# A hybrid encoder block: twelve late tiles of its input projection as six pairs of seven products

## The chip, the cores and the metric

The kernel runs on one core of a Trainium2 chip. The metric is the device time of one launch in microseconds (us), as the median of several runs. The engines are named as the profile names them: PE is TensorE's matmuls and PEld its weight loads, DVE is VectorE, ACT is ScalarE, POOL is GpSimd, SP issues most DMAs. A suffix q (SPq) is the engine's queue.

## The reference, cut to what matters

```python
hn = rmsnorm(concat(meta_tokens, x), norm_in_g)      # 16 + 512 rows, 2048 wide
P = hn @ w_in                                        # 2048 x 8320: r, k, v, g, two low ranks, B, C, h, gc
Pr = Pr + (prev - Pr) * mu_shift                     # r, k, v, g and the low ranks only
y = rwkv7_recurrence(r, decay, k, v, kk, kk * a)     # 16 heads of 64, chunks of 64 frames
y_a = (groupnorm(y) + bonus) * silu(g)
y_b = B * causal_conv3(C * h) * silu(gc)             # 1024 channels
out = rmsnorm(h_res + concat(y_a, y_b) @ w_out, norm_f_g)[16:]
```

Everything is float32.

## The kernel before

**The input projection.** Weights are cut into 65 tiles of 128 output columns: one for the low ranks, eight each of r, k, v, g, B, C, h and gc. `plan` lists them in the order in which TensorE takes them; the last sixteen are C, h, B, gc for i = 4 to 7. Float32 products are made from float32r parts: a value is split into a high part (a cast) and a low part (the value less its high part), and three matmuls, high x high, high x low and low x high, stand for one product. The activations, scaled by the norm's gain, lie split in `xh` and `xl`, 16 blocks (kt) of 128 inputs by 528 frames. One tile is 16 blocks by three matmuls for every range of frames (`steps`, L346). B and gc take the 512 real frames in one matmul; C and h need two frames more for the convolution and take them as 258 + 256 columns.

**Weights.** A tile is loaded as two halves of 512 KB (`prefetch`, L166) into a ring of three `raw` buffers. A half is two quarters of 512 columns. `split_w` makes a quarter's parts: ScalarE casts (L158), VectorE or GpSimd subtracts (L159; of every half one quarter each, from the twelfth half on). The parts go to a ring of six buffers, `hl`.

**The order.** TensorE's order is written out by hand. `mains` is a generator that yields after every matmul of the projection; the recurrence and what prepares it call `fill(ns)`, which takes matmuls from it for as many ns as the kernel counts (0.43 ns a column). So every step of the recurrence is followed by projection matmuls that fill the time until its result is there; the lengths stand in the table `FW`. `later(ns, fn)` puts off DMA issues by the same clock. The order on VectorE, ScalarE and GpSimd is the framework's scheduler's, with `tc.high_priority` and `tc.issue_after` as hints; each engine then runs its own list in order.

**Recurrence.** For pairs of heads, `prepare` and `invert` make the operands of the chunked recurrence, and `recur` runs nine chunks. In a chunk z (L996) goes through ScalarE as pn (L1004), is multiplied again (L1013), copied as u by ScalarE and VectorE (L1016, L1017), and gives outputs and the next state (L1048, L1052; L1060 and L1061 on VectorE). The fills behind the three steps are p, u and s. `norm` normalises a chunk's output (L1077 to L1089, with a power on GpSimd, L123).

**The end.** After the recurrence, `split_mix` loads and gates the 16 tiles of the mix (L1141) and splits them (L1146, L1147), and `sums` (L1157 to L1160) makes sums of its quarters, between the last four tiles of the projection. The output projection (L1285) is made of seven products of quarter matrices instead of eight, in the form of Strassen and Winograd: the sums of the mix on one side (`split_form`, L1202 and L1203), sums of the weights on the other (`add`, L1246, or by DMA), split by `split_unit` (L1255, L1256).

## Time and profile before

| | |
|---|---|
| median of three runs | 1000.38 us (1000.17 to 1001.08) |
| the profiled execution | 1001.71 us, span 999.9 us |
| PE, PEld busy | 988.3, 911.6 us |
| DVE, ACT, POOL busy | 685.7, 394.6, 271.5 us |
| DMA | 174.8 MB, mean 175 GB/s |
| mean granted TensorE clock | 0.997 |

Times in the views are us from the span's start. A group's row gives the line, the engine, the operation, output<-inputs with their shapes, the count, then busy time in us and the mean of one instruction in ns, then the engine's idle time in front and what ended it. A timeline row gives start, length and instruction. Matmuls overlap in the array, so that one lasts longer than its distance to the next.

### The profile page before, as it was taken

How to read it: one execution, taken by the hardware profiler on the slowest of the kernel's cores; microseconds unless marked ns; L12 is line 12 of the kernel's file. 1: busy time of each engine (PE TensorE's matmuls, PEld its weight loads, DVE VectorE, ACT ScalarE, POOL GpSimd, SP SyncE). 2: the span in 40 equal slices, each digit the busy share in tenths (PEclk: the TensorE clock that was granted, in tenths of full speed). 3: DMA queues.
4: the chain of work that ended last, by engine and by line, in shares of the span. 5: the costliest groups of instructions: out<-in, count | busy, mean ns of one | idle time of the engine just before them, and what ended most of it. 6: DMA issues, size and time to landing. Idle time of an engine off the chain costs nothing.

```text
span 999.9 us, 23699 instructions
## 1 busy us (share of the span) xinstructions
PE 988.3 (99%) x9723; PEld 911.6 (91%) x9723; DVE 685.7 (69%) x1247; ACT 394.6 (39%) x729; POOL 271.5 (27%) x292
## 2 busy tenths in 40 slices
PE   9999999999999999999999999999999999999996
PEld 7999999999998999998999998889889898888885
DVE  6777965588765679744669644244554697997897
ACT  7553433344313434322434322222232426546463
POOL 0122423234233424232324222223332333001001
PEclk9999999999999999999999999999999999999998
DMA  9525576555575373854274846877673688797654
GB/s 329 148 85 148 132 207 171 153 144 145 141 189 165 95 193 98 203 149 119 85 197 108 197 136 192 297 215 241 204 226 99 174 264 210 187 318 175 160 127 168
DMA packets 185036, 174.82 MB, mean 175 GB/s; under 512 B 121568, under 2 KB 142816, under 8 KB 184416
## 3 DMA queue, kind: packets, MB, share of 16 engines
q1 hardware_dynamic: 182336, 164.40, 57.2%
q0 software_dynamic: 2304, 8.39, 4.8%
q8 instruction: 76, 1.25, 0.5%
q10 hardware_dynamic: 288, 0.52, 0.1%
q14 instruction: 32, 0.26, 0.1%
HBM read 136.92 MB, written 36.35 MB: 173 GB/s over the span
## 4 chain that ended last, share of the span: by engine, by line
PE 90%; DVE 5%; DMA 2%; issue 1%; SPq 0%; ACT 0%; POOL 0%; DVEq 0%; ACTq 0%; POOLq 0%
PE ps_v L346 9%; PE ps_k L346 9%; PE ps_h L346 9%; PE ps_g L346 9%; PE ps_r L346 9%; PE ps_B L346 9%; PE ps_gc L346 9%; PE ps_C L346 8%; PE M L1285 5%; PE P L1285 2%; DVE o L1256 2%; PE g L703 2%; PE Q L1285 1%; PE zs L1048 1%; PE ps_lora L346 1%
## 5 line engine op out<-in xcount | busy, mean ns | idle before, releaser
L158 ACT CAST w<-wr 128x512 fp32r<-128x512 f32 x252 | 153.0, 619 | 285.4 <-PE ps_C L346 47.3
L159 POOL TENSOR_TENSOR w<-wr,w 128x512 fp32r<-128x512 f32 x119 | 169.1, 1422 | 346.6 <-ACT w L158 289.4
L159 DVE TENSOR_TENSOR w<-wr,w 128x512 fp32r<-128x512 f32 x133 | 98.6, 747 | 114.5 <-ACT w L158 114.2
L346 PE MATMUL ps_k<-xh,w 128*128 128x272 f32 (+1 forms) x512 | 95.3, 284 | 0.0
L346 PE MATMUL ps_v<-xh,w 128*128 128x256 f32 (+1 forms) x512 | 95.3, 284 | 0.0
L346 PE MATMUL ps_r<-xh,w 128*128 128x258 f32 (+1 forms) x512 | 94.4, 281 | 0.0
L346 PE MATMUL ps_h<-xh,w 128*128 128x256 f32 (+1 forms) x512 | 94.0, 282 | 0.0
L346 PE MATMUL ps_C<-xh,w 128*128 128x256 f32 (+1 forms) x512 | 93.1, 281 | 0.0
L346 PE MATMUL ps_g<-xh,w 128*128 128x256 f32 (+1 forms) x512 | 91.5, 280 | 0.0
L346 PE MATMUL ps_B<-xh,w 128*128 128x512 f32 x256 | 83.8, 395 | 0.0
L346 PE MATMUL ps_gc<-xh,w 128*128 128x512 f32 x256 | 81.3, 392 | 0.0
L346 PEld LDWEIGHTS ps_k<-xh,w 128*128 128x128 f32 x512 | 80.0, 188 | 0.4
L346 PEld LDWEIGHTS ps_v<-xh,w 128*128 128x128 f32 x512 | 80.0, 188 | 0.3
L346 PEld LDWEIGHTS ps_h<-xh,w 128*128 128x128 f32 x512 | 79.2, 188 | 0.7
L346 PEld LDWEIGHTS ps_r<-xh,w 128*128 128x128 f32 x512 | 79.6, 188 | 0.1
L346 PEld LDWEIGHTS ps_C<-xh,w 128*128 128x128 f32 x512 | 79.2, 188 | 0.6
L346 PEld LDWEIGHTS ps_g<-xh,w 128*128 128x128 f32 x512 | 78.7, 188 | 0.2
L346 PE MATMUL ps_k<-xl,w 128*128 128x272 f32 (+1 forms) x256 | 72.6, 284 | 0.0
L346 PE MATMUL ps_v<-xl,w 128*128 128x272 f32 (+1 forms) x256 | 72.5, 283 | 0.0
L346 PE MATMUL ps_h<-xl,w 128*128 128x258 f32 (+1 forms) x256 | 71.8, 281 | 0.5 <-issue 0.5
L346 PE MATMUL ps_g<-xl,w 128*128 128x258 f32 (+1 forms) x256 | 72.0, 281 | 0.0
L346 PE MATMUL ps_r<-xl,w 128*128 128x258 f32 (+1 forms) x256 | 72.0, 281 | 0.0
(337 smaller groups left out, 2265.3 us busy)
## 6 DMA issues: line engine op xcount, KB each, us to landing
wr<-in_w_in_dram SPq DMA_DIRECT2D x126, 512.0 KB
ct<-opd SPq DMA_DIRECT2D x64, 288.0 KB
wo<-in_w_out_dram SPq DMA_DIRECT2D x24, 512.0 KB
x<-in_w_out_dram POOLq DMA_DIRECT2D x16, 512.0 KB, 6.1
opd<-ar SPq DMA_DIRECT2D x8, 576.0 KB
opd<-gt SPq DMA_DIRECT2D x16, 288.0 KB
opd<-bt SPq DMA_DIRECT2D x64, 64.0 KB
x<-in_w_out_dram SPq DMA_DIRECT2D x8, 512.0 KB
```

Source lines behind the costliest of these rows:

```text
L158: nc.scalar.copy(hi, rq)
L159: low[q] = eng.tensor_tensor(out=lo, in0=rq, in1=hi.bitcast(F32), op=ALU.subtract).ins
L346: nc.tensor.matmul(ps[r], ww[:, w], xx[:, kt, a:b], start=(kt == 0 and n == 0), stop=(kt == KT - 1 and n == 2))
L703: nc.tensor.matmul(z[h][:, c - c0], bk[hs, c, h : h + 2, :].rearrange("p a s -> p (a s)"), ar[hs, c].rearrange("p a s -> p (a s)"), start= ...
L1048: nc.tensor.matmul(d[hs, j], w, x[hs], start=(a == 0), stop=(a == b - 1))
L1256: last = nc.vector.tensor_tensor(out=lo, in0=rq, in1=hi.bitcast(F32), op=ALU.subtract)
L1285: nc.tensor.matmul(bank[s], left(prod, jj, m, s), w, start=(jj == 0 and n == 0), stop=(jj == 7 and n == 2))
```

## The change

Of the last sixteen tiles, C, h, B and gc for i = 4 to 6 are taken as six pairs, (C, h) and (B, gc). A pair is a product of 2 x 2 quarters: two tiles of outputs, two halves of the 2048 inputs, two halves of the 512 frames. Instead of eight products of quarters, seven are made, each of 8 blocks by 256 or 258 frames: M1, P5, Q6, M3, M7, M2, P4. Four of them have sums of weight quarters, made in place in the raw buffers; four have sums of activations. Banks of PSUM are used twice within a pair: after M1 its value is copied out and Q6 is added onto it, and so on. The results are put together from the copies and banks by ScalarE and VectorE.

The activation sums are made early in the projection, one block of eight after the other, stored in DRAM (`fsum`), and loaded and split before the recurrence. The third of them (M7's) is written over the second half of frames in `xh` and `xl` for the first eight blocks (`third_form`), and undone after the last M7 (`restore`). For that the frames lie in two segments, with two frames twice.

Beside that: `raw` becomes four named buffers in pairs; parts of the weights in a pair are dealt out to VectorE and GpSimd by a table, and after the last pair all low parts of the input weights are GpSimd's; the product and first tap of the convolution go to VectorE for i from 4 on; both copies u go to ScalarE and overwrite pn; several buffers of the recurrence are single instead of double; the fills p, u and s are shorter; in the output projection some form splits are put behind weight splits on VectorE; the framework's scheduler is asked to order by its timeline (`schedule_with_timeline_sim=True`); the mix stage begins once `restore` is issued.

```diff
-    tr=3200, ..., p=2900, u=2900, s=5200, last=3700, mix=2600,
+    tr=3200, ..., p=2300, u=2500, s=4200, last=3700, mix=2600, form=1000, split=6000, early=60000, apart=48000,
...
+ON_POOL = {   # (low part, sum): which halves of a product's weights GpSimd makes
+    "M1": ((), ()), "P5": ((), ()), "Q6": ((), ()), "M3": ((0, 1), ()), "M7": ((0, 1), (0, 1)), "M2": ((0, 1), ()),
+    "P4": ((0, 1), (0, 1)),
+}
+PAIRS = (("C", "h", 4), ("B", "gc", 4), ("C", "h", 5), ("B", "gc", 5), ("C", "h", 6), ("B", "gc", 6))
...
+        for prod, r, extra in (
+            ("M1", X, None), ("P5", X, Y), ("Q6", X, Z), ("M3", Z, None), ("M7", Y, Z), ("M2", W, None), ("P4", X, W)
+        ):
+            slots += [(("pair", u, (prod, q)), r, 512 * q, extra) for q in range(2)]
...
+    def engines(n):
+        kind = slots[n][0]
+        if kind[0] != "pair":
+            late = n > LAST_PAIR
+            return nc.gpsimd if (n % 2 or late) and 22 < n < S_IN else nc.vector, None
+        low_on, sum_on = ON_POOL[kind[2][0]]
+        return (nc.gpsimd if kind[2][1] in low_on else nc.vector), (nc.gpsimd if kind[2][1] in sum_on else nc.vector)
...
+    def advance(upto, more=0):          # in place of prefetch
...
+                if extra is not None:
+                    sum_eng.tensor_tensor(out=x, in0=x, in1=held[extra][:, o : o + 512], op=ALU.add)
+                split_w(n, x, low_eng)
...
+    def pair(u):
...
+        def product(which, ps, n, begin=False):
+            advance(state["used"] + 8, 3)
+            for q in range(2):
+                hi, lo = quarters["pair", u, (which, q)]
+                for k in range(4):
+                    h, l = left[which][4 * q + k]
+                    w = slice(k * P, (k + 1) * P)
+                    for m, (ww, xx) in enumerate(((hi, h), (hi, l), (lo, h))):
...
+        yield from product("M1", A, HALF, True)
+        copy(m1, A, HALF)
+        yield from product("P5", B, n_t, True)
+        copy(v, B, n_t)
+        yield from product("Q6", A, n_t)
+        copy(u2, A, HALF)
+        yield from product("M3", B, HALF)
+        with ahead():
+            nc.vector.tensor_tensor(out=u2[:, 0:HALF], in0=B[:, 0:HALF], in1=u2[:, 0:HALF], op=ALU.subtract)
+        yield from product("M7", A, n_t)
+        with ahead():
+            nc.vector.tensor_tensor(out=v[:, 0:n_t], in0=v[:, 0:n_t], in1=A[:, 0:n_t], op=ALU.subtract)
+        if len(units) == u + 1 or len(units[u + 1]) == 1:
+            restore()
+        use(*t2, (u2, v))
+        C = pm.tile([P, 512], F32, tag=f"m{c}", name=f"ps_{name}_C")
+        yield from product("M2", C, HALF, True)
+        with ahead():
+            nc.vector.tensor_tensor(out=m1[:, 0:HALF], in0=C[:, 0:HALF], in1=m1[:, 0:HALF], op=ALU.add)
+        yield from product("P4", A, n_t)
+        use(*t1, (m1, A))
...
+    def early_form(k):
+        t = temporary(k, f"rows{k}", [P, 2, 2, W2])
+        for n, kt in enumerate((k, KA + k)):
+            nc.sync.dma_start(t[:, n].rearrange("p h l -> p (h l)"), xt[:, kt, META:XW])
...
+                    nc.scalar.activation(t[:, n], t[:, n], AF.Copy, scale=gain[:, kt : kt + 1])
...
+                nc.gpsimd.tensor_tensor(out=o, in0=a, in1=b, op=op)     # four sums
...
+            nc.sync.dma_start(fsum[:, k, 0:4:3], t[:, 0])
+            nc.sync.dma_start(fsum[:, k, 1:3], t[:, 1])
...
+    def third_form():
+        for j in range(0, KA, 2):
+            apart(xh[:, j : j + 2, T0X:XW], xl[:, j : j + 2, T0X:XW], thirds[j // 4][:, j % 4 : j % 4 + 2], nc.vector)
+
+    def restore():
...
+        for j in range(0, KA, 2):
+            t = tm(f"again{j}")[:, 0 : 2 * n].rearrange("p (k l) -> p k l", k=2)
+            nc.sync.dma_start(t, xt[:, j : j + 2, T0X:XW])
+            for k in (j, j + 1):
...
+                nc.scalar.activation(hi, x, AF.Copy, scale=g)
+                nc.vector.scalar_tensor_tensor(
+                    out=lo, in0=x, scalar=g, in1=hi.bitcast(F32), op0=ALU.mult, op1=ALU.subtract
+                )
...
-            u = ch.tile([P, 2, 4, CH], F32, tag="u", name=f"u{c}", bufs=2)
+            u = pn
             with ahead():
                 nc.scalar.copy(u[:, 0], z[0][:, 1])
-                nc.vector.tensor_copy(u[:, 1], z[1][:, 1])
+                nc.scalar.copy(u[:, 1], z[1][:, 1])
...
     with tc.tile_pool(name="ch", bufs=1, side="right", reuse_waits="tile") as ch:
         recur(ch)
+    while "restored" not in state:
+        step()
...
-    with tile.TileContext(nc) as tc:
+    with tile.TileContext(nc, schedule_with_timeline_sim=True) as tc:
```

429 lines of the change are left out of this document (314 added, 115 removed).

## The prediction

> **What bounds the kernel now.** I read the page first: which engine is full, and at what clock.
>
> ```profile
> PE 988.3 (99%) x9723; PEld 911.6 (91%) x9723; DVE 685.7 (69%) x1247; ACT 394.6 (39%) x729; POOL 271.5 (27%) x292
> PEclk9999999999999999999999999999999999999998
> ```
>
> TensorE is busy for 988.3 of 999.9 us at full clock. Busy alone does not say that it works without gaps, so the view of waits for PE comes next; its longest entry, and the one that matters later:
>
> ```profile
> PE pwarm L207 <- DVE cold L204: 1.4, 1, 1.4
> ...
> PE M L1285 <- DVE o L1256: 0.4, 1, 0.4
> ```
>
> So TensorE hardly waits for anybody: work taken from it shortens the run, as long as the other engines keep up with what is left. The chain of waits shows where they barely do. Its columns are start, length, what.
>
> ```profile
> 782.71 10.88 PE ps_gc L346 x48
> 793.59 11.39 PE ps_C L346 x96
> 804.98 11.21 PE ps_h L346 x96
> 816.19 10.90 PE ps_B L346 x48
> 827.09 10.90 PE ps_gc L346 x48
> 838.01 0.69 DVE gc L373
> ...
> 874.48 5.51 PE M L1285 x23
> ```
>
> Until 838 the chain lies on TensorE's tiles. From 838 to 874 it lies on VectorE, and in front of 874 TensorE waits its 0.4 us. At that place VectorE has no reserve: whatever reaches 838 late on VectorE, TensorE pays. By stretches (PE, PEld, DVE, ACT, POOL, clock, DMA share, GB/s):
>
> ```profile
> 620.00:778.00 158.00, 157.11 (x2865) 140.53 (x2864) 72.26 (x124) 42.46 (x81) 47.30 (x41) 1.00 0.68 213
> 778.00:838.00 60.00, 60.00 (x358) 53.56 (x357) 46.51 (x62) 20.80 (x38) 22.67 (x15) 1.00 0.81 233
> 838.00:875.00 37.00, 36.52 (x159) 29.50 (x159) 36.14 (x46) 23.48 (x38) 3.49 (x4) 1.00 0.72 184
> ```
>
> The recurrence (first row) leaves VectorE half idle; behind it, VectorE fills 46.5 of 60 us, and then 36.1 of 37.
>
> **The products.** Twelve tiles, three each of C, h, B and gc, go from eight quarter products per pair of tiles to seven. A product is 24 matmuls, eight groups of three. One timeline row of a h tile stands for the middle matmul of a group, so its distance to the same row three groups on is three groups:
>
> ```profile
> 690.09 0.28 PE L346 MATMUL ps_h<-xl,w 128*128 128x258 f32 x1
> ...
> 691.16 0.28 PE L346 MATMUL ps_h<-xl,w 128*128 128x258 f32 x1
> ...
> 691.52 0.28 PE L346 MATMUL ps_h<-xl,w 128*128 128x256 f32 x1
> ...
> 692.54 0.28 PE L346 MATMUL ps_h<-xl,w 128*128 128x256 f32 x1
> ```
>
> A group takes 1.07/3 = 0.357 us at 258 columns and 1.02/3 = 0.340 at 256; a product 2.85 or 2.72. A C-h pair has four products of the first kind and three of the second, 19.6 us, in place of 11.39 + 11.21 = 22.6. A B-gc pair has seven at 2.72, 19.0 us, in place of 21.8. Three of each: 3 x 3.0 + 3 x 2.8 = 17.4 us. One eighth of 133.2 us, which is the pure count, is 16.7. I take 17.0.
>
> The pairs halve the width of B's and gc's matmuls from 512 to 256 columns, with twice the weight loads for each column. By the rows this is free: 48 matmuls of 512 columns in 10.90 us are 0.227 each, and a 256-column one is 0.340/3 = 0.113. The Trainium skill speaks against it: TensorE: Matmul & The Clock Gate, Back-to-back issue gap, gives a sustained spacing of 81 ns at 128 columns and 131 ns at 512, from which I would estimate 98 ns at 256; a B-gc pair would then go from 96 x 131 ns = 12.6 to 168 x 98 ns = 16.5 us, and the three pairs of each kind together would be some 4.5 us slower. The trace does not agree with that spacing.
>
> **What the pairs cost the other engines.** Each pair has 14 half-products of weights instead of 8 quarters, each with a cast on ScalarE and a subtraction for the low part, and 8 sums of weight quarters in front. The subtractions and sums are dealt out as 10 to VectorE and 12 to GpSimd (before: 4 and 4). From the groups between 614 and 800 us:
>
> ```profile
> L159 POOL TENSOR_TENSOR w<-wr,w 128x512 fp32r<-128x512 f32 x25 | 32.6, 1305 | 95.0 <-ACT w L158 83.3 <-issue 7.1 <-DMA ct<-opd 4.4
> L158 ACT CAST w<-wr 128x512 fp32r<-128x512 f32 x51 | 31.6, 619 | 86.6 <-PE ps_h L346 26.8 <-PE ps_C L346 21.3 <-PE ps_B L346 16.4
> L159 DVE TENSOR_TENSOR w<-wr,w 128x512 fp32r<-128x512 f32 x25 | 17.1, 683 | 27.0 <-ACT w L158 26.9
> L123 POOL TENSOR_TENSOR nv<-nv,mhalf 128x8 f32<-128x8 f32 x8 | 13.1, 1643 | 0.7
> ```
>
> ScalarE: 14 x 0.62 = 8.7 us a pair, plus three bank copies; against 19 us or more this is covered. GpSimd: 12 x 1.3 = 15.6 us a pair, with 19.0 to 19.6 of products, or 30 where the recurrence is woven in. It fits, but these two engines are not independent. VectorE in a row, and GpSimd at the same time:
>
> ```profile
> 798.01 0.68 DVE L159 TENSOR_TENSOR w<-wr,w 128x512 fp32r<-128x512 f32 x1
> 798.62 0.41 DVE L1147 TENSOR_TENSOR m<-mix,m 128x256 fp32r<-128x256 f32 x1
> 798.95 0.74 DVE L1141 SCALAR_TENSOR_TENSOR mix<-mix,hl,rb 128x512 f32<-128x512 f32 x1
> 799.61 0.68 DVE L1147 TENSOR_TENSOR m<-mix,m 128x512 fp32r<-128x512 f32 x1
> 800.22 0.74 DVE L1141 SCALAR_TENSOR_TENSOR mix<-mix,hl,gg 128x512 f32<-128x512 f32 x1
> 800.88 1.78 DVE L1141 SCALAR_TENSOR_TENSOR mix<-mix,hl,rb 128x512 f32<-128x512 f32 x1
> ...
> 812.38 1.22 DVE L1159 SCALAR_TENSOR_TENSOR mix<-mix,mix 128x1024 f32<-128x1024 f32 x1
> 813.52 0.42 DVE L1147 TENSOR_TENSOR m<-mix,m 128x256 fp32r<-128x256 f32 x1
> ...
> 819.08 0.42 DVE L373 TENSOR_TENSOR hh<-ps_h,rs 128x258 f32<-128x258 f32 x1
> ```
>
> ```profile
> 800.35 1.76 POOL L159 TENSOR_TENSOR w<-wr,w 128x512 fp32r<-128x512 f32 x1 [4.68 <-ACT w L158]
> ...
> 818.60 1.71 POOL L159 TENSOR_TENSOR w<-wr,w 128x512 fp32r<-128x512 f32 x1 [2.38 <-ACT w L158]
> ```
>
> The VectorE instruction at 800.88 takes 1.78 us instead of 0.74, and ends when GpSimd's (800.35 + 1.76 = 802.11) is over and its own work done; GpSimd's is longer too. The one at 819.08, which reads a PSUM bank, stays at 0.42 inside GpSimd's 818.60. I read this as one path that both need when VectorE has two operands in SBUF: the two kinds of work add up. GPSIMD Reference, 8. Key points, in the Trainium skill, says the same: GpSimd shares its SBUF interfaces with VectorE and collides with instructions of two SBUF inputs. The trace agrees, 1.78 against 0.74 us.
>
> So I keep a joint account. From the starts in a row, VectorE needs 0.61 us for a 512-wide two-operand subtraction, 0.33 for 256, 0.66 for a scaled one, 1.14 for 1024; GpSimd 1.3.
>
> *Pairs inside the recurrence.* By the built order of TensorE the nine chunks run from M7 of the first pair to P4 of the fifth: 4.2 pairs, 2.1 chunks a pair. A chunk starts at 694.30 and the next at 711.51 (rows under the fills, below), 17.2 us, of which the three fills take 11.0 by the kernel's count and a tenth more in fact (it counts 0.43 ns a column, the 258-wide rows take 0.46, and a fill ends on a whole matmul): 5.1 us are the chunk's own matmuls. A pair then lasts 19.3 + 2.1 x 5.1 = 30.0 us. Account: GpSimd 15.6, half a gate product 0.6; VectorE's weights 10 x 0.61 = 6.1; scaling and convolution of the two outputs, three 256-wide and three 512-wide instructions in the mean of both kinds of pair, 2.8; two 512-wide per chunk, 2.6. Sum 27.7 of 30.0: covered, with little play. With six weight buffers the split may run three products ahead, which evens out short excesses. Each bank is read out while another product of 2.7 us runs; the last readout (M7 before P4) stands on VectorE behind the normalisation's product, which stands behind GpSimd's power (1.64 us). Between 0 and 1.5 us a pair; I take 0.5, together 2.
>
> *The last pair*, B6-gc6, runs after the recurrence: 19.0 us for 15.6 on GpSimd and a power of 1.6, while VectorE ends h6's convolution and the last normalisation (some 4 us). Between 0 and 5; 2.
>
> *Shorter fills* of the recurrence (p 2.9 to 2.3, u 2.9 to 2.5, s 5.2 to 4.2). For a chunk, ScalarE, VectorE and PE:
>
> ```profile
> 695.50 0.66 ACT L1004 ACTIVATE pn<-rz 128x256 f32<-128x256 f32 x2 [1.86 <-PE rz L996]
> ...
> 699.51 0.37 ACT L1016 COPY u<-rz 128x256 f32<-128x256 f32 x1 [1.73 <-PE rz L1013]
> ```
>
> ```profile
> 706.09 0.69 DVE L1061 TENSOR_TENSOR st<-st,dd 128x512 f32<-128x512 f32 x1
> ```
>
> ```profile
> 694.30 0.34 PE L996 MATMUL rz<-st,ct 64*64 64x64 f32 x8
> ...
> 698.78 0.69 PE L1013 MATMUL rz<-pn,ct 64*64 64x64 f32 x32
> ...
> 702.76 0.28 PE L1048 MATMUL zs<-u,ct 64*64 64x64 f32 x2
> ...
> 711.51 0.34 PE L996 MATMUL rz<-st,ct 64*64 64x64 f32 x8
> ```
>
> pn is ready at 696.16 and read at 698.78, 2.6 us later; u at 699.9, or 700.3 when both its copies go to ScalarE, read at 702.76; the state at 706.8, read at 711.5. The fills lose 0.6, 0.4 and 1.0. Covered: 0, unless casts that wait stand in front.
>
> *Activation sums.* Eight times two loads, two scalings on ScalarE, four half-wide GpSimd instructions and two stores, spread over some 400 us in which these engines are under half used: 0. Loading them back and splitting them (eight casts and subtractions of 774 columns) falls beside the last inversion; four casts stand on ScalarE in front of that inversion's own copies. 0 to 2; I take 0.5.
>
> *The end of the projection.* Between M7 of the last pair and the end of gc7 lie two products and four tiles: 5.4 + 44.4 = 49.8 us. Into it fall, on VectorE: undoing the third sum (8 x 0.33 = 2.6), half tiles of b6 and gc6 and their gate (2.2), seven 512-wide and eight 256-wide subtractions of the mix (6.9), 18 scaled instructions (11.9), four sums (4.6), h7's convolution that comes over from GpSimd and ScalarE (1.2), one weight sum (1.1), six output weights (3.7): 34.2. GpSimd now makes all 16 low parts of C7 to gc7 instead of half of them, and two gate products: 18 x 1.3 = 23.4. Sum 57.6 in 49.8: if the path is used alternately, VectorE comes to gc7's end 7.8 us late. The same account for before, from the first split of the mix at 790 to 838: 33 and eight GpSimd instructions (of the 15 from 778 on), 10.4, are 43.4 in 48. Nothing hides this, since behind it VectorE is the chain. Against the full amount: some of GpSimd's instructions run beside PSUM reads, and TensorE's waits in the last pair lengthen the window. From 0 to 8; I take 4, the middle, as no row is nearer to either end.
>
> **The sum.** 2 + 2 + 0.5 + 4 = 8.5 us given back of 17.0. The profiled execution took 1001.71 us with a span of 999.9: it comes to 993.2. The median of the three runs, 1000.38, is 1.3 below it: 992.
>
> **Rivals.** *All covered*: the play in buffers hides every term; 1000.4 - 17 + 1.5 = 985. For it: TensorE waits 3 us in all now, with VectorE full from 838. Against it: 57.6 in 49.8. *The tail gives it back*: 8 there, 5 in the last pair, 3 in the others: 1000.4 - 17 + 16 = 999. *Slower*: the joint path binds in the pairs too. It decides once 12 GpSimd instructions and 12.1 us of other work exceed 30.0, so from 1.49 us each; the contended rows show 1.71 and 1.76. At 1.75 a pair takes 33.1, 3.1 too long, times 4.2 is 13; the last pair 5 and the tail 8 with it: 1000.4 - 17 + 26 = 1009. Against it: in the recurrence the mean is 1.305. *The gain doesn't come, since the recurrence is a chain of latencies*: its fills are cut by 2.0 us a chunk, which casts standing in front of its copies turn into waits; nine times that is 18, and the time about 1001. Against it: the 2 to 4.7 us of play above. *Narrow matmuls cost*: if the 256-wide ones took the 0.119 us of the 258-wide ones, 1008 of them are 120 us, a gain of 13 instead of 17: 996 with the same waits. By rows that is the most that the page's spacing rule could amount to here.
>
> **Chances.** Forecast (988 to 996) 0.45; all covered 0.25; the tail 0.13; slower 0.12; latencies 0.04; narrow 0.01. Outside 0.2% (2 us, about what a measurement of this kernel can tell from no change): faster 0.45 + 0.25 + 0.01 + half the tail = 0.77; same, the rest of the tail and most of the latencies, 0.10; slower 0.13. The range of 984 to 1001 leaves out the slower rival and a little of the best case.
>
> **What would show it.** Right: pairs whose products step by 2.7 to 2.9 us; 23 or more us of GpSimd between C7 and gc7; a wait of M1 or P5 of the output projection for VectorE of about 4 us, where 0.4 is now. Wrong: TensorE's waits under 3 us in all (covered), or products in the pairs that wait for GpSimd's low parts by more than 0.5 us each (slower).

## The result and the profile after

The changed kernel takes 1041.35 us (median of 4 runs, 1039.73 to 1042.6), the kernel before 1000.73 beside it (4 runs, 1000.17 to 1001.47): a ratio of 1.0405, 95% interval 1.0385 to 1.0424. Forecast were 992 us with a range of 984 to 1001. The sign was wrong.

The page of the profiled execution (1039.73 us, span 1037.8):

```profile
PE 1000.6 (96%) x9867; PEld 932.3 (90%) x9867; DVE 760.1 (73%) x1325; ACT 444.1 (43%) x824; POOL 385.0 (37%) x376
...
PEclk9999999999999999999999999999989998999999
```

TensorE has become busier (988.3 before), though an eighth of the matmul work of twelve tiles is gone, and it is idle for 37 us instead of 12: of the 37.9 us by which the spans differ, 25.6 are idle time of TensorE and 12.3 are busy time. The view of waits for PE, its largest entries (total, times, longest):

```profile
PE rz L1286 <- issue: 9.0, 3, 4.6
PE M L1583 <- DVE gc L641: 7.0, 1, 7.0
PE zy L1342 <- issue: 2.6, 2, 1.8
PE t L1225 <- DVE xm L1212: 2.2, 1, 2.2
```

The time is best divided by five stretches: up to the first matmul of C3, to that of C4 (where the pairs begin), to that of C7 (where they end), to the end of gc7, and the rest. Before (columns PE, PEld, DVE, ACT, POOL, clock, DMA share, GB/s):

```profile
20.00:566.00 546.00, 545.98 (x5116) 527.13 (x5116) 383.64 (x768) 212.79 (x393) 168.36 (x190) 1.00 0.57 149
566.00:614.70 48.70, 48.70 (x547) 43.64 (x546) 24.53 (x48) 14.14 (x25) 13.02 (x10) 1.00 0.56 154
614.70:793.40 178.70, 177.81 (x2977) 158.59 (x2976) 82.58 (x137) 49.71 (x93) 54.50 (x46) 1.00 0.68 212
793.40:838.00 44.60, 44.60 (x290) 40.80 (x289) 39.48 (x54) 15.43 (x30) 16.76 (x10) 1.00 0.85 246
838.00:999.90 161.90, 153.34 (x696) 127.01 (x695) 143.21 (x216) 88.81 (x159) 16.92 (x22) 0.98 0.68 188
```

And after:

```profile
20.00:577.30 557.30, 557.26 (x5115) 537.72 (x5114) 372.88 (x752) 223.59 (x408) 199.05 (x222) 1.00 0.59 159
577.30:631.10 53.80, 51.57 (x547) 45.56 (x546) 43.23 (x82) 22.54 (x37) 16.77 (x10) 0.97 0.71 204
631.10:817.10 186.00, 170.57 (x3121) 163.23 (x3120) 138.36 (x193) 74.15 (x153) 121.04 (x89) 0.96 0.63 200
817.10:864.70 47.60, 46.16 (x290) 41.23 (x288) 45.52 (x50) 16.03 (x32) 26.15 (x17) 1.00 0.90 253
864.70:1037.80 173.10, 156.49 (x697) 129.13 (x696) 147.52 (x224) 93.38 (x164) 20.13 (x25) 0.96 0.69 191
```

The differences are +11.3, +5.1, +7.3, +3.0 and +11.2, together 37.9 us, as the spans differ. Forecast were 0, +0.5, -13 (-17 + 2 + 2), 0 and +4. No stretch is as forecast, and three readings follow.

**The first stretch** holds the same matmuls, TensorE waits nowhere in it and its clock is full; yet it is 11.3 us longer. So matmuls that the change seems to leave alone became slower. In the timeline of a g tile, each row `xl` is three matmuls from the next. Before:

```profile
249.83 0.28 PE L346 MATMUL ps_g<-xl,w 128*128 128x256 f32 x1
...
250.17 0.28 PE L346 MATMUL ps_g<-xl,w 128*128 128x256 f32 x1
```

After:

```profile
254.83 0.28 PE L446 MATMUL ps_g<-xl,w 128*128 128x256 f32 x1
...
255.90 0.28 PE L446 MATMUL ps_g<-xl,w 128*128 128x256 f32 x1
```

Before, three take 0.34 us, 113 ns each; after, nine take 1.07 us, 119 each. Over the whole stretch the median of a 256-column step (from the start of a matmul to the start of the next) goes from 113 to 119 ns (some 1700 steps), of a 512-column one from 227 to 234, while 258 columns stay at 120 and 272 at 126 to 127. A likely cause is what the diff does to the tiles that these read: `LX`, the pitch of a row of `xh` and `xl`, goes from 576 to 544 columns, and the second half of the frames starts at column 274 instead of 272.

**The pairs.** TensorE computes for 170.6 us instead of 177.8, but the stretch is longer. VectorE has little reserve left. It is busy for 138.4 us, and in the five largest entries of its own waits in this stretch it waits for 31 us for GpSimd, transfers and ScalarE, and for 10 us for TensorE itself. These are the first two:

```profile
DVE yc L1379 <- POOL nv L134: 18.8, 8, 3.0
DVE wr L250 <- DMA wr<-in_w_in_dram: 7.3, 3, 3.3
```

So 170 of 186 us are VectorE's work and what that work waits for from the side. One place shows how TensorE comes to wait for it (timeline of VectorE; the bracket is the wait in front):

```profile
753.79 0.42 DVE L541 TENSOR_TENSOR sums_B_gc<-ps_B_gc_C,sums_B_gc 128x256 f32<-128x256 f32 x1
756.70 0.69 DVE L250 TENSOR_TENSOR wr<-wr,wr 128x512 f32<-128x512 f32 x1 [2.48 <-DMA wr<-in_w_in_dram]
757.31 1.52 DVE L632 TENSOR_TENSOR gc<-sums_B_gc,rs 128x256 f32<-128x256 f32 x1
758.75 1.75 DVE L223 TENSOR_TENSOR w<-wr,w 128x512 fp32r<-128x512 f32 x1
760.54 1.63 DVE L250 TENSOR_TENSOR wr<-wr,wr 128x512 f32<-128x512 f32 x1
762.10 0.68 DVE L1350 TENSOR_TENSOR st<-zs,st 128x512 f32<-128x512 f32 x1
```

The last of TensorE's `zs` matmuls of the chunk:

```profile
753.42 0.22 PE L1338 MATMUL zs<-ct 64*64 64x64 f32 x2
```

The state that needs them is added up at 762.10, behind a weight sum that waits 2.48 us for a transfer, and behind three more instructions of 1.5 to 1.75 us that take 0.4 to 0.7 elsewhere. The next chunk's `rz` waits 4.6 us for it. What such a wait costs shows in the clock (PE, PEld, DVE, ACT, POOL, clock):

```profile
759.00:763.60 4.60, 0.03 (x1) 0.03 (x1) 4.53 (x5) 0.62 (x1) 2.62 (x2) 0.76 0.82 278
763.60:768.20 4.60, 4.60 (x74) 4.42 (x75) 4.53 (x9) 2.68 (x7) 1.81 (x2) 0.50 0.02 4
768.25:771.00 2.75, 2.75 (x50) 2.55 (x50) 1.95 (x2) 1.67 (x4) 2.59 (x3) 1.00 0.00 0
871.75:877.40 5.65, 5.65 (x13) 4.42 (x14) 4.50 (x6) 4.09 (x6) 0.87 (x1) 0.50 1.03 216
877.50:881.00 3.50, 3.50 (x17) 2.90 (x16) 3.50 (x5) 3.02 (x5) 0.00 (x0) 1.00 1.06 273
```

Behind the wait of 4.6 us TensorE runs at half the clock for another 4.6 us, and then at the full one: 2.3 us lost on top. Behind the wait of 7.0 us for gc (last two rows) it is 5.7 us at half, 2.9 lost. The trace has two more such places: 3.4 us at half the clock behind the wait of 2.2 us for xm, and 4.9 us behind another wait of rz, of 3.8 us. Together the four waits are 17.6 us, and the clock behind them costs some 9.3 more.

**Behind gc7** that wait and its clock are most of the 11.2 us. VectorE reaches gc's scaling 6 us after the bank is ready:

```profile
865.02 0.68 DVE L641 TENSOR_TENSOR b<-ps_B,rs 128x512 f32<-128x512 f32 x1
867.14 1.29 DVE L223 TENSOR_TENSOR w<-x,w 128x512 fp32r<-128x512 f32 x2 [1.44 <-ACT w L222]
869.01 1.98 DVE L223 TENSOR_TENSOR w<-x,w 128x512 fp32r<-128x512 f32 x3 [0.58 <-ACT w L222]
870.90 0.69 DVE L641 TENSOR_TENSOR gc<-ps_gc,rs 128x512 f32<-128x512 f32 x1
```

It is late with B7's tile, and five subtractions of output weights stand in front of gc. For 2.0 of the 6 us it waits in between for ScalarE's casts of these weights, and ScalarE in turn for their transfer:

```profile
866.49 1.14 ACT L222 CAST w<-x 128x512 fp32r<-128x512 f32 x2 [2.42 <-DMA x<-in_w_out_dram]
868.36 1.14 ACT L222 CAST w<-x 128x512 fp32r<-128x512 f32 x2 [0.73 <-DMA x<-in_w_out_dram]
```

So VectorE's own load is not all of this wait.

### The profile page after: what moved, and what is told of

Same layout as the page of the kernel before. It is cut to its first block, busy times and chain, and to the rows that moved or that the text cites. A ratio compares the mean times of both kernels' runs of the same rounds, so it can differ in the third digit from the quotient of the medians.

```text
span 1037.8 us, 24404 instructions
## 1 busy us (share of the span) xinstructions
PE 1000.6 (96%) x9867; PEld 932.3 (90%) x9867; DVE 760.1 (73%) x1325; ACT 444.1 (43%) x824; POOL 385.0 (37%) x376
## 5 line engine op out<-in xcount | busy, mean ns | idle before, releaser
L222 ACT CAST w<-wr 128x512 fp32r<-128x512 f32 x288 | 175.3, 618 | 281.8 <-PE ps_k L446 50.4
L223 POOL TENSOR_TENSOR w<-wr,w 128x512 fp32r<-128x512 f32 x151 | 223.0, 1487 | 192.7 <-ACT w L222 170.9
L223 DVE TENSOR_TENSOR w<-wr,w 128x512 fp32r<-128x512 f32 x137 | 103.0, 755 | 43.7 <-ACT w L222 43.2
L250 POOL TENSOR_TENSOR wr<-wr,wr 128x512 f32<-128x512 f32 x24 | 35.5, 1485 | 72.9 <-DVE w L223 25.7
L1538 POOL DMA_DIRECT2D x<-in_w_out_dram x16 | 14.2, 890 | 123.0 <-DVE o L1552 119.2
L446 PE MATMUL ps_h<-xh,w 128*128 128x258 f32 (+1 forms) x320 | 58.9, 283 | 0.0
L446 PE MATMUL ps_C<-xh,w 128*128 128x258 f32 (+1 forms) x320 | 58.7, 282 | 0.3 <-POOL w L223 0.3
L446 PE MATMUL ps_B<-xh,w 128*128 128x512 f32 x160 | 53.7, 401 | 0.0
L446 PE MATMUL ps_gc<-xh,w 128*128 128x512 f32 x160 | 52.9, 408 | 0.0
L446 PEld LDWEIGHTS ps_C<-xh,w 128*128 128x128 f32 x320 | 50.0, 189 | 0.5 <-POOL w L223 0.5
```

Source lines behind the costliest of these rows:

```text
L222: state["cast"] = nc.scalar.copy(hi, rq).ins
L223: low[n] = eng.tensor_tensor(out=lo, in0=rq, in1=hi.bitcast(F32), op=ALU.subtract).ins
L250: sum_eng.tensor_tensor(out=x, in0=x, in1=held[extra][:, o : o + 512], op=ALU.add)
L446: nc.tensor.matmul(ps[r], ww[:, w], at_(xx, kt, a, b), start=(kt == 0 and n == 0), stop=(kt == KT - 1 and n == 2))
L1538: nc.gpsimd.dma_start(chain[g], rows_of(half, k, col, g), accum_op=ALU.add)
```

## The experiments

Results in us, each beside the kernel before on the same chip (medians 1000.9 to 1001.3):

| run | median (4 runs) | ratio, 95% interval |
|---|---|---|
| b_lx544 | 1011.1 | 1.0099, 1.0084 to 1.0114 |
| b_shift2 | 1018.6 | 1.0177, 1.0160 to 1.0194 |
| b_w16 | 1009.3 | 1.0081, 1.0064 to 1.0098 |
| b_sched | 1019.1 | 1.0178, 1.0163 to 1.0193 |
| a_t280 | 1038.8 | 1.0375, 1.0357 to 1.0393 |
| a_w32 | 1040.6 | 1.0399, 1.0380 to 1.0417 |
| a_lx576 | 1041.1 | 1.0392, 1.0366 to 1.0418 |
| a_lx576p | 1034.6 | 1.0329, 1.0308 to 1.0351 |
| a_nopairs | 1028.0 | 1.0265, 1.0250 to 1.0280 |
| a_nopf | 1021.5 | 1.0203, 1.0188 to 1.0218 |
| a_nopf576 | 1013.0 | 1.0110, 1.0089 to 1.0131 |
| a_nosum | 1021.0 | 1.0191, 1.0175 to 1.0207 |
| a_selfsum | 1039.0 | 1.0375, 1.0358 to 1.0392 |
| a_swap | 1034.0 | 1.0327, 1.0310 to 1.0345 |
| a_late | 1038.0 | 1.0362, 1.0347 to 1.0378 |
| a_swlate | 1031.9 | 1.0306, 1.0291 to 1.0321 |
| a_fills | 1042.7 | 1.0410, 1.0388 to 1.0432 |
| a_sched | 1045.5 | 1.0447, 1.0430 to 1.0464 |

Names with b are edits of the kernel before, names with a of the changed one. An edit of the changed kernel lets the scheduler order the engines' lists anew, so it can move other instructions too: in the profiles of a_late, a_fills and a_nosum C3 starts at 581.9, 580.3 and 579.9 us instead of 577.3, with 2.1 to 2.5 us of idle TensorE in front of it.

### The place of the activations and weights

```diff
 b_lx544:
-LX = 576
+LX = 544
 b_shift2 (xl likewise):
-    xh = xp.tile([P, KT, LX], F32R, name="xh")
+    xh = xp.tile([P, KT, LX], F32R, name="xh")[:, :, 2 : 2 + L]
 a_t280 (with what follows from it in loads and scales):
-T0X = META + HALF + 2
+T0X = META + HALF + 8
 a_w32:
     if what == "pair":
-        return 16
+        return 32
```

> The kernel before with only the pitch of a row of xh and xl taken over from the changed kernel, 544 columns instead of 576; where the column ranges start (16, 14, 0, 272) stays. Theory A, the start of the second column range: the changed kernel moved it from column 272 to 274, eight bytes off the 32-byte grid on which it lay, and that alone makes a 256-column matmul step by 119 ns instead of 113. Then nothing happens here: the v, k, r and g tiles keep their 113 to 114 ns, 1000 to 1001 us. Rival B, the pitch: a row of 2176 instead of 2304 bytes is what costs. Then the 256-column matmuls step by 119 ns here, some 2350 of them, 14 us, and the 512-column ones by 233 instead of 227, 4 us more: about 1016 us.

> The kernel before with all of xh and xl moved by two columns, eight bytes; the pitch stays 576 columns. The 256-column matmuls (2352) then read from eight bytes beyond the 32-byte grid, as in the changed kernel, and the 512-column ones (768) too. Theory A, the start of the range: 119 ns instead of 113 for the first, 14 us, and some 233 instead of 227 for the second, 5 us: 1014 to 1020 us. Rival B, the pitch: no change, 1000 to 1001 us. Rival C, neither start nor pitch but other work (sums and forms that use SBUF at the same time): no change in either of these two kernels, and the steps stay at 113.

> The changed kernel with the second half of the tokens at column 280 instead of 274 (six unused columns between the halves, pitch still 544): the start is then on the 32-byte grid again. Theory A: the 256-column matmuls of k, v, r, g, C and h come back from 119 to 113 ns, and the C3 tile starts about 11 us earlier, near 566 us instead of 577; the time falls by 11 to 14 us, to 1027 to 1031 us. Rival B, pitch, or rival C, other work: no change, 1041 us and the C3 tile near 577. The pairs keep their waits in either case.

> The changed kernel with the parts of the pairs' weights 32 instead of 16 columns into their buffers, as the k, v and lora tiles have them; nothing else. In the pairs 256-column matmuls step by 118 to 119 ns even where their activations lie on the 32-byte grid (M1, M2). Theory D: for 256 columns the place of the weights against that of the activations counts too (the tiles of before with 113 ns have both at the same place in 128 bytes modulo 64, the weights at 32); then M1 and M2 fall to 113 ns, some 280 matmuls by 6 ns, about 2 us of time. Rival E: the step in the pairs is the lower granted clock there (0.94 to 0.97): no change, 1041 us within 2 us and the same steps.

Each of the two costs time by itself: the pitch 10.1 us, a start moved by eight bytes 17.5. So rival C, other work, is not needed. (b_shift2 moves every range, the changed kernel only the second half of the frames; no run puts the pitch and the start of the changed kernel together into the kernel before.) In b_shift2 TensorE hardly waits, and every stretch up to gc7 is longer with the same matmuls:

```profile
20.00:578.80 558.80, 558.80 (x5114) 539.11 (x5114) 384.19 (x767) 212.62 (x392) 168.06 (x190) 1.00 0.56 146
...
628.30:808.40 180.10, 179.67 (x2977) 159.53 (x2976) 83.09 (x138) 49.47 (x93) 54.31 (x46) 1.00 0.68 211
```

The 256-column step is 118 ns in b_lx544 and 119 in b_shift2. Theory A in its first form (a start on the 32-byte grid is enough) fell with a_t280, which has it and stays at 118 ns. a_w32 moved nothing. Theory E does not explain its steps: with the stretches at half the clock left out, the pairs' 256-column median is 119 ns in a_w32 and in the changed kernel. It does not refute theory D either, since its pitch is 544 columns. If not the activations' place alone, is it the place against that of the weights?

```diff
 b_w16:
-    return 32 if what in (...) or part in AT_32[what][i] else 64
+    return 16 if what in (...) or part in AT_32[what][i] else 48
 a_lx576 (pitch and place modulo 128 bytes as before; T0X = META + HALF + 32):
-        t = wp.tile([P, 2 * 512 + 64], F32R, tag="hl", name=name, bufs=6)
+        t = wp.tile([P, 2 * 512 + 64], F32R, tag="hl", name=name, bufs=5)
 a_lx576p: as a_lx576, and in front of xh
+    xp.tile([P, 32], F32, name="skip")
```

> The kernel before with the weights of all tiles but B and gc 16 columns (64 bytes) nearer to the start of their buffers (16 and 48 instead of 32 and 64); the activations stay. Theory D: the step of a 256-column matmul hangs on the place of activations and weights to each other, and the table of offsets in the kernel before is made for the pitch and the start it had; then 113 becomes 118 to 119 ns for some 2350 matmuls, and the time 1010 to 1014 us. Rival K: only the place of the activations counts: 1000 to 1002 us, 113 ns.

> The changed kernel with the activations placed as before: pitch 576 columns, the second half of the tokens at column 304, which lies at the same place modulo 128 bytes as column 272 did. The 4 KB that this takes come from the weight buffers, five instead of six. Theory A (the place of the activations costs, pitch and start together): the 256-column matmuls up to the C3 tile step by 113 to 114 ns again, C3 starts near 566 us, and the time falls by 11 to 16 us, to 1025 to 1030. Rival: with one weight buffer less the pairs wait longer, and what is won in front is lost there: C3 near 566, but 1035 to 1045 in all. Second rival, the sums of the activations and the new order of instructions cost in front and not the place: C3 stays near 577.

> The changed kernel with pitch 576, second half at column 304 and five weight buffers (1041.1 us, where only tiles whose weights lie at 32 modulo 256 bytes kept steps of 115), with all activations moved by another 128 bytes: the second half then lies at 96 modulo 256 bytes, as before, where in the kernel before weights at 32 and at 160 both give 113. Theory L, the rule is one modulo 256 bytes: all 256-column matmuls are at 113 to 114 again, up to C3 about 8 us are won, and the time is 1030 to 1035 us. If steps stay at 117, the rule is finer than that.

b_w16 leaves the activations where they were, moves only the weights by 64 bytes, and takes 8.4 us more; its 256-column step is 120 ns. So the weights' place counts as well as the activations', and the table `AT_32`, which puts weights 32 or 64 columns into their buffers, seems made for the pitch and starts of the kernel before. a_lx576 had a wrong expectation: the place modulo 128 bytes as before, yet 117 ns and no gain in time; tiles with weights 64 columns in had a median step of 116, those 32 columns in one of 118. Its five buffers cost too: TensorE is idle for 6.8 us between 20 us and C3, where in the changed kernel it is not. a_lx576p, moved by 128 bytes, gains 6.5 us on it. That is partly theory L, but weights 64 columns in are now the slow ones (118, against 114 at 32), where in the kernel before both had 113 to 114. That which weights are slow turns over when only the activations move shows that the two places count together. The rule that orders this is not found.

### Without the pairs

```diff
 a_nopairs:
-PAIRS = (("C", "h", 4), ("B", "gc", 4), ..., ("B", "gc", 6))
+PAIRS = ()
 a_nopf: also
-p=2300, u=2500, s=4200
+p=2900, u=2900, s=5200
 a_nopf576: also LX = 576, T0X = META + HALF
```

> The changed kernel without the six pairs: the twelve tiles are computed as before from eight quarter products, no sums of activations or weights are made, low parts alternate up to the end as before. What stays of the change: the place of the activations (pitch 544, second half at 274), the shorter fills of the recurrence, the scheduler that orders the instructions, and the banks. Theory A: this carries the loss in front and the same loss in the twelve tiles, as in the kernel before with the activations moved by two columns (1018.6 us): 1015 to 1020. Then the pairs themselves with all that hangs on them cost 1041 - 1018 = 23 us instead of saving 17. Rival, all loss lies in the pairs: about 1001. Rival, the order and the shorter fills cost as well: above 1025.

> The kernel without the pairs (1028.0 us), with the fills of the recurrence as long as before (2.9, 2.9 and 5.2 us instead of 2.3, 2.5 and 4.2). Without the pairs it lay 10 us above the kernel before with the activations moved by two columns (1018.6), 6.5 of them between the C4 and the C7 tile. Theory I: the shorter fills cost, the recurrence's copies and state come later than their readers; then the stretch from C4 to C7 falls from 186.6 to 180 us and the time to 1020 to 1023. Rival J: the order of the instructions that the scheduler makes costs; then nothing changes, 1027 to 1029.

> The kernel without pairs and with the long fills (1021.5 us), with the activations placed exactly as before too: pitch 576, second half at column 272, six weight buffers. Of the change stay the order that the scheduler makes, the banks and the split of 530 columns. Theory A (the place of the activations): 256-column matmuls step by 113 ns, C3 starts near 566, and the time is 1001 to 1004 us. Rival J, the scheduler's order: above 1006.

Without pairs the kernel still loses 27 us (1028.0 instead of theory A's 1015 to 1020, as the last rival had it): the pairs with what hangs on them cost 13.4, not 40. Its stretch from C4 to C7 is as long as that with the pairs, since the recurrence, with shorter fills, now holds TensorE up. It waits once for 2.1 us and once for 2.8, and behind the second its clock is halved:

```profile
627.60:814.20 186.60, 181.73 (x2977) 161.14 (x2976) 90.52 (x149) 51.31 (x104) 52.20 (x43) 0.99 0.71 218
...
759.90:763.20 3.30, 3.30 (x9) 2.52 (x9) 1.09 (x2) 0.40 (x1) 0.00 (x0) 0.50 0.00 0
```

With the old fills (a_nopf) the stretch is 180.3, and 6.5 us come back, as theory I had it. The old place on top (a_nopf576) brings C3 from 578.4 to 568.3 and steps of 114 ns, and 8.5 us in the median (13.4 up to C7, of which 4.6 go again behind gc7). But 1013.0 is not the 1001 to 1004 of theory A: 12 us were left. Taken one after the other, these runs divide the loss: 13.4 us pairs, 6.5 fills, 8.5 place, and 12 for what is left of the change, the scheduler's order, the banks and the single buffers among it.

### The scheduler's order

```diff
 b_sched:
-    with tile.TileContext(nc) as tc:
+    with tile.TileContext(nc, schedule_with_timeline_sim=True) as tc:
 a_sched: the same line undone
```

> The kernel before with only the order of the instructions off TensorE made by the scheduler that the changed kernel uses (its own simulated timeline) instead of the default one; TensorE's order is the same. Without pairs, with long fills and the old place of the activations the changed kernel still took 1013.0 us, 12 more than before. Theory J: that is the scheduler's order, so 1009 to 1014 us here, with C3 at about 568 and some 5 us more behind gc7. Rival M: it is what else stayed of the change (banks, the split of the activations): 1000 to 1004.

> The changed kernel with the scheduler's default order instead of the one from its simulated timeline. Theory J: what the order costs without the pairs is saved here too, 5 to 12 us: 1029 to 1036. Rival N: the order was chosen for the pairs, and the default one puts weight sums and casts in front of the recurrence's copies, or the other way round: 1041 to 1060, slower by waits of rz and zs.

The order alone costs the kernel before 17.9 us, more than theory J asked for. C3 starts at 570.1 instead of 566.0, and the stretch behind gc7 is most of the rest:

```profile
843.10:1016.60 173.50, 158.38 (x696) 129.73 (x695) 143.73 (x217) 90.01 (x159) 17.79 (x23) 0.96 0.66 182
```

That is 173.5 us instead of 161.9 for the same matmuls: TensorE is busy for 5.0 us more, at a mean clock of 0.96 instead of 0.98, and idle for 6.6 more. So the order is enough for the 12 us left in a_nopf576, but no run takes it out of that kernel, and a share of the banks and buffers is not excluded. In the changed kernel it is the other way round, as rival N had it: the default order loses another 4.2 us. Its stretch from C3 to C4 is 49.7 us instead of 53.8 and that behind gc7 168.2 instead of 173.1, but the pairs take 197.0 instead of 186.0.

### The weights' work in the pairs

```diff
 a_nosum:
-                if extra is not None:
-                    sum_eng.tensor_tensor(out=x, in0=x, in1=held[extra][:, o : o + 512], op=ALU.add)
 a_selfsum:
-                    sum_eng.tensor_tensor(out=x, in0=x, in1=held[extra][:, o : o + 512], op=ALU.add)
+                    sum_eng.tensor_tensor(out=x, in0=x, in1=x, op=ALU.add)
 a_swap:
-    "M1": ((), ()), "P5": ((), ()), "Q6": ((), ()), "M3": ((0, 1), ()), "M7": ((0, 1), (0, 1)), ...
+    "M1": ((0, 1), ()), "P5": ((0, 1), (0, 1)), "Q6": ((0, 1), (0, 1)), "M3": ((), ()), ... all others ((), ())
```

> The changed kernel without the 48 sums of weights in front of the pairs' casts (P5, Q6, M7 and P4 are computed with one of the two matrices only); transfers, casts, low parts and products stay. Theory F: VectorE's queue stands behind a weight sum that waits for a late transfer, and the recurrence's state behind it; without the sums the waits of rz (9.0 us in all) and most of the gaps inside the pairs go, and the pairs take some 165 to 170 instead of 186 us: 1020 to 1027 us. Rival G, casts and subtractions are the load, and the sums only a third of it: half of that, 1030 to 1035. If 1038 or more, the sums and their wait are not the cause.

> The changed kernel with the weights' work dealt out the other way round: the sums and low parts of P5 and Q6 and the low parts of M1, whose matrices come last, go to GpSimd (10 instructions a pair), those of M3, M7, M2 and P4 to VectorE (12). The volume on the two engines together is the same. Theory F (VectorE's queue stands behind a sum that waits for a transfer): the wait is then in GpSimd's queue, where the state of the recurrence is not; the waits of rz fall from 9.0 us to under 3, and the time by 5 to 12 us, 1029 to 1036. Rival G (the common path of VectorE and GpSimd is simply full): no change or a little slower, 1040 to 1045. Rival H: GpSimd's powers stand behind the waiting sums and VectorE's normalisation behind these, so the block comes back by another way: 1041 or above, with VectorE waiting for nv instead of the transfer.

> The changed kernel in which each weight sum adds a matrix to itself instead of to the second one: the same number of sums of the same size on the same engines, but none waits for the transfer of a second matrix (P5, Q6, M7 and P4 are computed from one matrix). Without any sums the time was 1021.0 us, 20 us less; dealt out the other way round 1034.0. Theory F (the wait for the late transfer in VectorE's queue): most of the 20 us come back here too, 1022 to 1030, and the waits of rz go. Rival G (the volume of the sums on the path that VectorE and GpSimd share): 1037 to 1042, waits of rz stay. In between: both, in the proportion that shows.

Without the sums 20.3 us go: in the profiles 14.6 in the pairs and 8.0 behind gc7, where the wait for gc is 1.0 instead of 7.0, while the other stretches lose 4. The pairs' stretch falls to 171.4, and VectorE is no longer full:

```profile
632.50:803.90 171.40, 165.82 (x3121) 159.73 (x3120) 105.48 (x173) 78.38 (x160) 87.77 (x69) 0.99 0.70 225
```

I had taken this for theory F. a_selfsum refuted it as it was put: with the same sums, none of them waiting for a second matrix, 2.3 us are won, hardly more than the measurement can tell. The waits of rz go, as F says, but another takes their place. Waits for PE in a_selfsum:

```profile
PE ps_C_h_A L508 <- DVE sums_C_h L534: 9.9, 2, 5.2
...
PE ps_B_gc_A L508 <- DVE sums_B_gc L534: 3.8, 3, 1.4
```

and VectorE's own, in the pairs:

```profile
DVE yc L1379 <- POOL nv L134: 34.2, 8, 8.5
```

VectorE's normalisation waits for GpSimd's power, which stands in GpSimd's queue behind low parts and sums; behind it on VectorE stands the readout of a bank that TensorE needs (L534, at 716.47). The longest case in a_selfsum, GpSimd first:

```profile
706.74 2.04 POOL L250 TENSOR_TENSOR wr<-wr 128x512 f32<-128x512 f32 x2 [3.29 <-DMA wr<-in_w_in_dram]
...
712.86 1.65 POOL L134 TENSOR_TENSOR nv<-nv,mhalf 128x8 f32<-128x8 f32 x1
```

```profile
714.54 0.69 DVE L1379 TENSOR_TENSOR yc<-yc,nv 128x512 f32<-128x512 f32 x1 [8.50 <-POOL nv L134]
```

What shows is a queue in order that passes lateness on, whichever instruction has it. The lateness has two sources here. Between VectorE's statistics and the power stand two sums and three low parts, 5.8 us of work (rival G), and the first of the sums waits 3.3 us for the transfer of its own matrix. In the other long wait, of 8.1 us, GpSimd's sum waits 4.1 us in the same way. So theory F's transfer came back in GpSimd's queue, and as a_selfsum keeps the transfers, and a_nosum removes the volume and the waiting sums together, the share of each stays open. a_swap deals out the same volume so that GpSimd has less: it is busy for 96.6 us instead of 121.0, and VectorE's wait for the power is 4.8 instead of 18.8 us. The waits of rz fall from 9.0 to 2.4 and 7.4 us are won, both as theory F forecast, but not for its reason: VectorE waits longer for the transfers, not shorter. In the pairs 7.1 us go. Behind gc7, where the wait is now 0.9, another 8.2 go, but 6.5 of them come back between C7 and gc7, where TensorE waits 4.3 for the undoing of the third sum. VectorE's waits in the pairs in a_swap:

```profile
DVE wr L250 <- DMA wr<-in_w_in_dram: 11.9, 2, 6.6
...
DVE yc L1379 <- POOL nv L134: 4.8, 5, 1.2
```

### Fills and the low parts at the end

```diff
 a_fills:
-p=2300, u=2500, s=4200
+p=2900, u=2900, s=5200
 a_late:
-            return nc.gpsimd if (n % 2 or late) and 22 < n < S_IN else nc.vector, None
+            return nc.gpsimd if n % 2 and 22 < n < S_IN else nc.vector, None
 a_swlate: a_late and a_swap
```

> The changed kernel with the fills of the recurrence as long as before (2.9, 2.9 and 5.2 us). Theory I: TensorE has more to do before it reads the state, and the waits of rz (9.0 us) shrink to under 4: 1031 to 1037 us. Rival F: the state stands behind a sum that waits for a transfer, and 2 us more of filling for a chunk hide only part of a wait of up to 4.6 us: 1037 to 1040. Rival: the recurrence then needs more work than the pairs have beside it and runs on into the last tiles, with its normalisations in front of the mix: 1041 or above.

> The changed kernel with the low parts behind the last pair (C7, h7, B7, gc7) dealt out alternately to VectorE and GpSimd as before, instead of all 16 to GpSimd. The first matmul behind gc7 waits 7.0 us for VectorE's gc. By the joint account of the two engines, eight instructions of 1.3 to 1.8 us on GpSimd are replaced by eight of 0.61 on VectorE, 6 to 9 us less on their common path: the wait falls to 0 to 3 us, and the time by 4 to 8 us, to 1033 to 1037. Rival: the load is VectorE's own; then it grows by 8 times 0.65 = 5 us, the wait is 7 to 12 us and the time 1041 to 1046.

> The changed kernel with two cures together: the weights' work of the pairs dealt out the other way round (alone 1034.0 us) and the low parts behind the last pair alternately on VectorE and GpSimd (alone 1038.0). If the two act in different places: 1041.4 - 7.4 - 3.4 = 1030.6. If the wait behind gc7 (0.9 us left in the first of them) is all that the second can take: 1033 to 1034. Slower than before in either case, by the place of the activations (some 17 us), the forms, and what is left of the waits.

Longer fills change nothing that can be told (the intervals overlap), so the 1031 to 1037 us of theory I did not come: the waits of rz fall from 9.0 to 2.8 us as theory I says, and the first matmul behind gc7 waits 11.5 instead of 7.0. a_late halves the wait of 7.0, to 3.5 us, the stretch behind gc7 is 4.7 us shorter, and the median gains 3.4: the direction of the joint account, a little under the 4 to 8 expected. Both cures together give 1031.9, between the sum (1030.6) and the smaller expectation: the best of the changed kernels that keep the pairs and compute the whole, 31 us above the kernel before. No run of the change is faster than the kernel before.

## Why the prediction was wrong, step by step

**Products, 17.0 taken.** The count was right; the duration was not. I took 0.340 us for three matmuls of 256 columns from the rows of before; in the pairs they step by 119 ns, 0.357. Where little holds TensorE up, it computes for 165.8 us in the pairs' stretch (a_nosum), against 177.8 in the kernel before and 179.7 without pairs at the same place (a_nopf): 12.0 or 13.9 saved. In the changed kernel 7.2 us of busy time are saved, and with 4.8 lost there to the halved clock that is 12.0 again. Both are near the 13 of the rival "narrow matmuls", to which I gave 0.01. The spacing in the Trainium skill (TensorE: Matmul & The Clock Gate, Back-to-back issue gap) finds no support here either: 512 columns step by 227 to 234 ns, not 131.

**What the sum left out: matmuls outside the pairs.** They were carried over at the durations of before, a term put at nothing without a word, and the diff's `LX` and `T0X` undid it. The first stretch lost 11.3 us; moving the activations by eight bytes costs the kernel before 17.5, and putting them back gains 8.5 without the pairs. The trace of before could not show it; a table of offsets by tile and part could have been read as a sign that places matter.

**Also left out: the scheduler's order.** It stood in the change and had no line in the sum; alone it costs the kernel before 17.9. With the pairs the same order saves 4.2 (a_sched).

**Pairs in the recurrence, 2 taken, and the last pair, 2.** Of the terms in the sum this one was furthest off. The stretch came out at 186.0 instead of the 165.7 that 178.7 - 17 + 4 gives: TensorE is idle in it for 15.4 us instead of 0.9, and the halved clock costs 4.8, so that it is 178.7 - 12.0 + 14.5 + 4.8. The account of 27.7 of 30.0 us took durations from a less crowded mix. Groups of VectorE in the stretch before:

```profile
L159 DVE TENSOR_TENSOR w<-wr,w 128x512 fp32r<-128x512 f32 x24 | 16.4, 684 | 27.0 <-ACT w L158 26.9
...
L1061 DVE TENSOR_TENSOR st<-st,dd 128x512 f32<-128x512 f32 x7 | 4.9, 703 | 0.2
```

And after:

```profile
L223 DVE TENSOR_TENSOR w<-wr,w 128x512 fp32r<-128x512 f32 x31 | 27.8, 898 | 1.8 <-ACT w L222 1.6
L250 DVE TENSOR_TENSOR wr<-wr,wr 128x512 f32<-128x512 f32 x20 | 16.2, 819 | 7.5 <-DMA wr<-in_w_in_dram 7.3
...
L1351 DVE TENSOR_TENSOR st<-st,dd 128x512 f32<-128x512 f32 x7 | 8.4, 1202 | 0.2
```

684 became 898 ns, and 703 became 1202, while GpSimd's busy share went from 30% to 65%: that fits the shared path. The rival "slower" named this mechanism, at 1.49 us a GpSimd instruction; the group after has 1.44 for low parts and 1.50 for sums, at the point from which it decides. I gave it 0.12. Its sign, products that wait for GpSimd's low parts, hardly came (two waits, of 1.1 and 0.6 us): it too missed how lateness became waits, by VectorE's queue in order, with the power and the late transfers in GpSimd's queue. I had named the readout behind the power and priced it at 0.5 us a pair. The Trainium skill, GPSIMD Engine Reference, 8. Key points, says that GpSimd shares its SBUF interfaces with VectorE, and these rows agree with it.

**Shorter fills, 0 taken.** They cost 6.5 us without the pairs, two waits of 2.1 and 2.8 us and 1.7 of halved clock, so the play of 2.6 us and more that I read from one chunk did not hold for all. With the pairs it cannot be told apart from zero, since what longer fills save is paid behind gc7.

**Activation sums, 0.5.** C3 to C4 is 53.8 us, 5.1 longer than before; it is 49.8 without pairs, but also 49.7 with pairs and the default order. So the work itself fits, and the order in which it stands costs: the inversion's t waits 2.2 us for VectorE's xm there, and the clock behind it 1.7 more.

**The end of the projection, 4 (0 to 8).** The wait was 7.0 us, in the range, and GpSimd's 26.2 us between C7 and gc7 are near the 23.4 taken. VectorE comes to gc's scaling 53.8 us after the start of C7; with the low parts dealt out (a_late) it is 49.0, and the wait is half. In a_swap, which leaves these low parts on GpSimd, it is 54.1 as well, and the wait is 0.9 only because TensorE is held up before. So the joint account holds here, except that 2.0 us of the lateness are a late transfer of output weights, which it did not have. What the step missed besides is the price of a wait: the 2.9 us of clock behind it. The Trainium skill, TensorE: Matmul & The Clock Gate, Part 1, says that an idle window of about 3.4 us takes the array to half its rate. The trace agrees in the rate (0.50 behind waits of 4.6 and 7.0 us), but shows it behind waits of 2.2 and, in a_nopairs, 2.8 us too, which are shorter than that. I had priced every wait at its length.

The signs that I had named for a right forecast all came: products of 24 x 0.119 = 2.86 us, GpSimd's 26.2 us, and the wait for VectorE, as 7.0 us instead of about 4. They could not tell it from what happened, since none looked at the matmuls outside the pairs or at the order.

Measured each for itself, the parts do not add up: place 17.5 and order 17.9 (each alone in the kernel before), fills 6.5 and pairs 13.4 (taken out of the changed one) are 55 us, and the difference is 40.6. Taken out one after the other they do (13.4, 6.5, 8.5 and a rest of 12), but then what a part costs depends on what is still there: with the pairs the order gives back 4.2 instead of costing 17.9.

## What to carry to other kernels

A sum of parts needs a line for what a change does to the instructions that it doesn't touch: operand places, instruction order. Rows of a resource are not prices for the same resource when it is more crowded. For an engine that takes its instructions in order, account what it waits for, and not only its busy time. A wait of TensorE costs more than its length here: 1.7 to 2.9 us more behind waits of 2.2 to 7.0 us.

## What was not expected of the hardware

- A 256-column matmul of 4-byte operands steps by 113 ns or by 117 to 120, and a 512-column one by 227 or 232 to 234, depending on where activations and weights lie in SBUF; 64 bytes of the weights are enough (b_w16), or 8 of the activations (b_shift2). 258 columns stay at 119 to 120 in all of these. What rule it follows stays open.
- The granted clock lies at 0.50 for 3.4 to 5.7 us behind a single wait of 2.2 to 7.0 us in the middle of a busy stretch. Behind a wait of 2.1 us in a_nopairs it stayed at 1.00.
